# Heads' stage of a hybrid decoder layer: results stored at once, their sums in the decay tiles of the ended scan, a third output gate buffer, gate pieces one tile later

## The chip, the cores and the metric

The kernel runs on one core of one Trainium2 chip. The metric is the device time of one execution in microseconds (us), taken as the median of three timed runs; lower is better. One further execution was taken with the hardware profiler, and every duration of a single instruction comes from that one.

A core has five engines that run their own instruction streams and wait for each other by semaphores: TensorE (PE in the profile; PEld is its weight load), VectorE (DVE), ScalarE (ACT), GpSimd (POOL) and SyncE (SP), which here issues nearly all DMAs. An engine takes its instructions in the order written down for it, so one that waits holds up all behind it.

## What is computed

The reference is one decoder layer on 512 tokens of width 2048 in float32. A normalized, conditioned input `h` is multiplied by one wide matrix `w_in`; its slices feed a sliding-window attention branch (a) and a gated DeltaNet branch (b), which are gated, added, and projected by `w_out`. The change lies in branch b. Cut to what matters:

```python
d_qkv = causal_conv_silu(d_qkv, conv_w)
dq, dk, dv = jnp.split(d_qkv, [DN_KEY, 2 * DN_KEY], axis=-1)
dq = jnp.repeat(l2_norm(dq...), rep, axis=2)      # 16 key heads, 32 value heads, 128 wide
dk = jnp.repeat(l2_norm(dk...), rep, axis=2)
o = gated_delta_rule(dq, dk, dv, g, beta)         # a scan over chunks with a 128x128 state per head
o = rms_norm(o, dn_norm_w) * jax.nn.silu(dz...)   # dz: the output gate
y_b = o.reshape(B, T, DN_VAL) @ w_o_dn            # 512x4096 by 4096x2048
y = jax.nn.sigmoid(mg_a) * y_a + jax.nn.sigmoid(mg_b) * y_b
return x + gate * (y @ w_out)                     # gate: c @ w_ada, last third
```

## The kernel before

**Matrix work.** Every float32 product is made of three passes of a rounded format (`mm3`, lines L275 to L277): the weights are split by ScalarE into a high part (`whi`, L53) and by VectorE into the rest (`wlo`, L54). `channel_tile` makes one tile of 128 channels by 512 tokens: 16 slices of the input's width, 48 matmuls, about 11 us. After every second slice it calls `pump`, eight times a tile.

**Side work.** All else is written as Python generators. `go` puts one among the live ones; every `pump` lets each live generator whose count has run out take its next step, and a `yield n` means "n pumps later" (`JOIN` in a yield puts the step beside another one's small matmuls). `beside(gen, rate, queue)` adds a queue that takes `rate` steps per pump. The program so written is then put in order for each engine by a list scheduler: an instruction can stand earlier or later than it was written, as its inputs are reckoned to be ready. `behind()` pins what is written inside it to a place after the latest matmul, without any wait on the chip.

**The heads' stage** runs from about 500 to 1650 us. `heads` (L889) takes the 16 key heads in turn, each with its pair of value heads, as five channel tiles: one of queries (`q`), two of values (`v`), two of the output gate (`z`). After the 16 pairs come two more channel tiles (`ma3`, `ma4`, part of the merge gates), then `drain_live`, which lets the last generators finish, then `drain` of the two side queues (L695 to L697).

- `queries` loads two decay tiles `E` (called `M` there; four buffers, 128 x 512 each) from `g_rows`, turns them into the masked decay, and multiplies them into the products of queries and keys; `values` transposes the values (`ptv`, L309).
- `scan` (L1010 on) runs the four chunks of the pair: `pp`, `r`, `pv`, `vn`, `vs`, `pd`, `S`, `po`. ScalarE copies `vn` (L1028) out of PSUM, VectorE scales it to `vs` (L1033), TensorE makes `pd` from it (L1041). The scan of one pair ends during the tiles of the next. Then the output is scaled (`osb`, L1077), transposed (`pto`) and multiplied into the gate tile (L1086): `z[e]` holds the result.
- `zgate` (L902) takes a gate tile `zh` from a ring of two buffers, writes it by ScalarE (L905), then makes `zth` (L907) and the silu (L909).
- `head_sums` (L1091) makes what the next stage needs. That stage multiplies by `w_o_dn` in seven block products instead of eight (a scheme of Strassen's kind), for which the four blocks of the left side (two heads, tokens 0 to 255 as `lo` and 256 to 511 as `hi`) and three sums of them, plus one that replaces a block, go to the scratch tensor `oq_d` in seven places. `od_order` says which product reads which place.

**The next stage** (`branch_b`) starts with two merge-gate tiles and then reads `oq_d` (`oraw`, L1123), splits it (`oh`, `ol`), and multiplies (`od`).

**The gate queue.** From the ninth pair (g = 8) on, the queue "gate" runs `gate` (L1653), which makes the vector `gate` of the reference: 32 pieces, each one VectorE operation over 1024 columns (L1670, L1672) with a load of 512 KB (`gw`) three pieces ahead, then four ends, each a load of `b_gate` (`gb`), a matmul (`pgate`, L1680), two VectorE operations (L1682, L1683) and a store. `heads` sets its rate: 0 in the query tile and the first value tile, 0.22 per pump in the second value tile and both gate tiles. From g = 2 on another queue ("ws") adds weight blocks in memory with large DMAs.

Of the kernel before, what the change touches and what calls it, by code (L numbers as in the profile page):

```python
# [7 lines left out]
F32 = mybir.dt.float32  # L8
# [3 lines left out]
ALU = mybir.AluOpType  # L12
# [4 lines left out]
P = 128  # L17
T = 512
# [19 lines left out]
class Layer:  # L38
# [670 lines left out]

    def od_order(self):  # L710
        return [
            ("m1", 0, (0, 0)), ("m2", 2, (1, 0)), ("m5", 4, None), ("m6", 5, None), ("m7", 1, None), ("m4", 3, None),
            ("m3", 6, (1, 1)),
        ]

# [173 lines left out]
    def heads(self, wk, g):  # L889

        st = {"z": []}
        for q in self.side.get("gate", []):
            q[1] = 0.0
        self.go(self.queries(wk, g, self.channel_tile(f"q{g}"), st), 0)
        for e in range(2):
            for q in self.side.get("gate", []) if e else []:
                q[1] = 0.22
            self.go(self.values(wk, g, e, self.channel_tile(f"v{2 * g + e}"), st), 0)
        for e in range(2):
            self.go(self.zgate(wk, self.channel_tile(f"z{2 * g + e}"), st), 0)  # L900

    def zgate(self, wk, ps, st):  # L902
        nc = self.nc
        zh = wk.tile([P, T], F32, tag="z", name="zh", bufs=2)
        nc.scalar.activation(zh, ps, AF.Copy, scale=self.dnwh)  # L905
        th = wk.tile([P, T], F32, tag="th", name="zth")
        nc.scalar.activation(th, ps, AF.Tanh, scale=0.5)  # L907
        yield 1
        nc.vector.scalar_tensor_tensor(out=zh, in0=th, scalar=1.0, in1=zh, op0=ALU.add, op1=ALU.mult)  # L909
        st["z"].append(zh)  # L910
# [95 lines left out]
    def scan(self, wk, g, k, kT, TT, qd, M, epsq, st):  # L1006
        nc = self.nc
# [5 lines left out]
        for c in range(NTB):  # L1013
            if c:
# [3 lines left out]
                for e in range(2):  # L1018
                    nc.vector.scalar_tensor_tensor(
                        out=r[:, e, :], in0=pp[:, e, :], scalar=self.neg_eg[:, c, 2 * g + e : 2 * g + e + 1],  # L1020
                        in1=v[e][:, c, :], op0=ALU.mult, op1=ALU.add,
# [8 lines left out]
            if c < NTB - 1:  # L1030
                vs = wk.tile([P, 2, P], F32, tag="vs", name="vs", bufs=1)
                for e in range(2):
                    nc.vector.tensor_scalar(  # L1033
                        out=vs[:, e, :], in0=vn[:, e, :], scalar1=self.kd[:, c, 2 * g + e : 2 * g + e + 1],
# [16 lines left out]
            if c < NTB - 1:  # L1051
# [3 lines left out]
                else:  # L1055
                    for e in range(2):
                        nc.vector.scalar_tensor_tensor(
                            out=Sn[:, e, :], in0=S[:, e, :], scalar=self.egl[:, c, 2 * g + e : 2 * g + e + 1],
                            in1=pd[:, e, :], op0=ALU.mult, op1=ALU.add,
# [4 lines left out]
        z = st["z"]  # L1064
# [4 lines left out]
        for e in range(2):  # L1069
            nc.vector.scalar_tensor_tensor(  # L1070
                out=ms[:, e, :], in0=osq[:, e, :], scalar=1.0 / P, in1=epsq, op0=ALU.mult, op1=ALU.add
# [3 lines left out]
        for e in range(2):  # L1075
            of = osb[:, e]
            nc.vector.tensor_tensor(  # L1077
                out=of, in0=of, in1=ro[:, e * NTB : (e + 1) * NTB].unsqueeze(2).to_broadcast([P, NTB, P]), op=ALU.mult
# [6 lines left out]
        for e in range(2):  # L1085
            nc.vector.tensor_tensor(out=z[e], in0=pts[e], in1=z[e], op=ALU.mult)  # L1086
            yield 1
        yield 5
        yield from self.head_sums(wk, g, z)

    def head_sums(self, wk, g, z):  # L1091

        nc = self.nc
        TT, STT = nc.vector.tensor_tensor, nc.vector.scalar_tensor_tensor
        lo, hi = slice(0, 256), slice(256, 512)
        s = wk.tile([P, 3, 256], F32, tag="sums", name="zs", bufs=1)
        TT(out=s[:, 0], in0=z[0][:, hi], in1=z[1][:, hi], op=ALU.subtract)
        STT(out=s[:, 1], in0=s[:, 0], scalar=-1.0, in1=z[0][:, lo], op0=ALU.mult, op1=ALU.subtract)
        yield 1
        TT(out=z[0][:, hi], in0=z[0][:, lo], in1=z[0][:, hi], op=ALU.add)  # L1100
        STT(out=s[:, 2], in0=s[:, 1], scalar=-1.0, in1=z[1][:, lo], op0=ALU.mult, op1=ALU.subtract)
        yield 3
        two = lambda x: x.rearrange("p (q t) -> p q t", q=2)
        for q, src in ((slice(0, 2), two(z[0])), (slice(2, 4), two(z[1])), (slice(4, 7), s)):
            nc.sync.dma_start(out=self.oq_d[q, g // 2].rearrange("q p k t -> p q k t")[:, :, g % 2, :], in_=src)


    def branch_b(self):
# [657 lines left out]
```

## Time and profile before

| what | us |
|---|---|
| median of three runs | 2892.06 |
| lowest and highest run | 2890.61, 2895.87 |
| the profiled execution | 2897.53 |
| its span, first to last instruction | 2895.8 |
| TensorE busy in it | 2832.1 |
| VectorE busy | 1875.7 |
| ScalarE busy | 1141.0 |

The time of an execution is its span and what lies around it, here 1.7 us. In a row of the timeline stand the start, the duration, the engine, the line of the kernel, the operation, the tiles (written <- read), the shapes, the number of instructions merged, and in brackets how long the engine stood idle before it and what ended that. In a row of waits stand who waited for whom, the total, the times, and the longest. "SPq" is SyncE issuing a DMA. Matmuls overlap in the pipeline, so the duration of one is longer than its share of the time.

### The profile page before, as it was taken

The numbers are of one execution on the slowest core, as the hardware profiler recorded it, in microseconds if no ns is written. First come the engines' busy times: TensorE is split into PE (matmuls) and PEld (weight loads), VectorE is DVE, ScalarE is ACT, GpSimd is POOL, SyncE is SP. The second block draws the span as 40 slices with busy tenths as digits, with TensorE's granted clock in tenths as the row PEclk, the third lists the DMA queues.
The fourth block names the chain that finished last, engine by engine and source line by source line (L and its number), as shares of the span: only waits on it lengthen the run. The fifth ranks groups of instructions, "written<-read, shape, count | busy, mean of one in ns | idle before, by whom it ended". The sixth has DMA issues, their size and how long they took to land.

```text
span 2895.8 us, 38255 instructions
## 1 busy us (share of the span) xinstructions
PE 2832.1 (98%) x14428; PEld 2328.1 (80%) x14428; DVE 1875.7 (65%) x3020; ACT 1141.0 (39%) x2161; POOL 281.8 (10%) x266
## 2 busy tenths in 40 slices
PE   8899999999999999999999999999999999999999
PEld 6677888888888788888878788888887788788787
DVE  6765898778787556666655456665555655554565
ACT  4354333433334333333333354443334434442343
POOL 0022111111111111111110000000100100000000
PEclk9999999999999999999999999999999999999999
DMA  9757564646667768878863377676645547365575
GB/s 386 289 164 206 168 183 144 207 129 218 189 203 207 232 197 265 242 241 235 250 171 107 130 252 264 241 249 208 219 152 162 160 152 213 124 226 179 188 232 168
DMA packets 205473, 590.09 MB, mean 204 GB/s; under 512 B 74564, under 2 KB 99652, under 8 KB 154088
## 3 DMA queue, kind: packets, MB, share of 16 engines
q1 hardware_dynamic: 195080, 529.44, 53.6%
q0 software_dynamic: 10208, 58.20, 10.3%
q8 instruction: 113, 1.85, 0.3%
q14 instruction: 72, 0.59, 0.1%
HBM read 523.79 MB, written 166.40 MB: 238 GB/s over the span
## 4 chain that ended last, share of the span: by engine, by line
PE 83%; DMA 4%; DVE 3%; issue 2%; ACT 1%; POOL 0%; SPq 0%; DVEq 0%; POOLq 0%; ACTq 0%
PE mm L275 19%; PE mm L277 19%; PE mm L276 19%; PE od L276 3%; PE od L275 3%; PE od L277 3%; DMA oq_d<-zh 2%; PE m L276 2%; PE m L277 2%; PE m L275 2%; PE S L1404 1%; PE po L1045 1%; PE O L1455 1%; PE pv L1026 1%; PE pP L309 1%
## 5 line engine op out<-in xcount | busy, mean ns | idle before, releaser
L275 PE MATMUL mm<-hh,whi 128*128 128x512 f32 x2784 | 1126.8, 405 | 2.3 <-ACT whi L53 1.6
L277 PE MATMUL mm<-hh,wlo 128*128 128x512 f32 x2784 | 1089.3, 391 | 1.1 <-DVE wlo L54 1.1
L276 PE MATMUL mm<-hl,whi 128*128 128x512 f32 x2784 | 1087.8, 391 | 0.0
L54 DVE TENSOR_TENSOR wlo<-raw,whi 128x1024 fp32r<-128x1024 f32 (+1 forms) x476 | 588.9, 1240 | 421.0 <-ACT whi L53 419.6
L53 ACT CAST whi<-raw 128x1024 fp32r<-128x1024 f32 (+1 forms) x476 | 496.8, 1047 | 776.3 <-PE mm L276 657.9
L275 PEld LDWEIGHTS mm<-hh,whi 128*128 128x128 f32 x2784 | 524.5, 188 | 115.2 <-issue 9.6
L277 PEld LDWEIGHTS mm<-hh,wlo 128*128 128x128 f32 x2784 | 523.2, 188 | 114.6 <-DVE wlo L54 1.9
L276 PEld LDWEIGHTS mm<-hl,whi 128*128 128x128 f32 x2784 | 524.7, 188 | 101.4 <-issue 1.4
L276 PE MATMUL od<-wlo,oh 128*128 128x512 f32 x448 | 174.5, 390 | 0.8 <-DVE wlo L54 0.8
L275 PE MATMUL od<-whi,oh 128*128 128x512 f32 x448 | 174.8, 391 | 0.0
L277 PE MATMUL od<-whi,ol 128*128 128x512 f32 x448 | 174.4, 389 | 0.0
L813 POOL TENSOR_TENSOR E<-E,neg_g 128x512 f32<-128x512 f32 x64 | 90.5, 1414 | 475.6 <-DMA E<-g_rows 339.2
L972 POOL TENSOR_TENSOR qe<-qe,yq 128x512 f32<-128x512 f32 x32 | 49.6, 1567 | 880.1 <-DMA qe<-eg_rows 654.4
L865 DVE TENSOR_TENSOR A<-A,atmp 128x62 f32<-128x62 f32 (+30 forms) x124 | 112.6, 908 | 1.4
L858 DVE TENSOR_TENSOR atmp<-A 128x62 f32<-128x62 f32 (+30 forms) x124 | 110.3, 890 | 1.3
L276 PEld LDWEIGHTS od<-wlo,oh 128*128 128x128 f32 x448 | 84.1, 188 | 18.2 <-DVE wlo L54 1.2
L277 PEld LDWEIGHTS od<-whi,ol 128*128 128x128 f32 x448 | 84.1, 188 | 17.5
L275 PEld LDWEIGHTS od<-whi,oh 128*128 128x128 f32 x448 | 84.1, 188 | 17.2
L54 DVE TENSOR_TENSOR wlo<-raww,whi 128x1024 fp32r<-128x1024 f32 x56 | 68.4, 1223 | 44.4 <-ACT whi L53 44.4
L53 ACT CAST whi<-raww 128x1024 fp32r<-128x1024 f32 x56 | 58.9, 1056 | 79.5 <-PE m L277 71.7
L1047 ACT COPY osb<-po 128x256 f32<-128x256 f32 x64 | 23.9, 373 | 149.7 <-PE po L1045 149.7
L1428 ACT ACTIVATE sm<-sm,mx,rs 128x256 f32<-128x256 f32 (+1 forms) x128 | 72.1, 565 | 3.3 <-DVE mx L1423 3.3
(341 smaller groups left out, 3288.7 us busy)
## 6 DMA issues: line engine op xcount, KB each, us to landing
raw<-in_w_ch SPq DMA_DIRECT2D x158, 1024.0 KB
wa<-in_w_ada_ss SPq DMA_DIRECT2D x32, 1024.0 KB
od_m<-in_w_od POOLq DMA_DIRECT2D x32, 1024.0 KB, 13.9
raw<-od_m SPq DMA_DIRECT2D x32, 1024.0 KB
raw<-in_w_od SPq DMA_DIRECT2D x24, 1024.0 KB
E<-g_rows SPq DMA_DIRECT2D x64, 256.0 KB
od_m<-in_w_od SPq DMA_DIRECT2D x16, 1024.0 KB
od_m<-od_m SPq DMA_DIRECT2D x16, 1024.0 KB
```

What stands on the lines that cost most here:

```text
L53: self.nc.scalar.copy(out=hi, in_=src)
L54: self.nc.vector.tensor_tensor(out=lo, in0=src, in1=hi.bitcast(F32), op=ALU.subtract)
L275: nc.tensor.matmul(ps, lhsT=wh, rhs=xh, start=first, stop=False)
L276: nc.tensor.matmul(ps, lhsT=wh, rhs=xl, start=False, stop=False)
L277: self.last_mm = nc.tensor.matmul(ps, lhsT=wl, rhs=xh, start=False, stop=last).ins
L309: self.small = self.nc.tensor.transpose(dst[:, c * P : (c + 1) * P], src_cols(c), self.ident).ins.name
L813: self.in_turn(nc.gpsimd.tensor_tensor(out=E, in0=E, in1=ng, op=ALU.add))
L858: eng.tensor_tensor(out=t, in0=A[:, m : m + 1, m + 1 :].to_broadcast([P, m, n]), in1=A[:, :m, m : m + 1].to_broadcast([P, m, n]), op=ALU.mult,
L865: eng.tensor_tensor(out=A[:, :m, m + 1 :], in0=A[:, :m, m + 1 :], in1=t, op=ALU.add)
L972: self.in_turn(nc.gpsimd.tensor_tensor(out=qf, in0=qf, in1=q, op=ALU.mult))
L1026: nc.tensor.matmul(pv[:, e, :], lhsT=TT[e][:, c, :], rhs=r[:, e, :] if c else v[e][:, c, :], start=True, stop=True)
L1428: nc.scalar.activation(t, t, AF.Exp, scale=r[:, h : h + 1], bias=mx[:, h : h + 1], accum_out=den[:, h : h + 1])
```

## The change

Four things change, all in the heads' stage.

1. `zgate` has three buffers for `zh`, not two.
2. `head_sums` stores at once, one pump step after the multiplications, what the next stage reads as it is: `z[0]`'s first half, and `z[1]`.
3. The sums are no longer made in a tile of their own and partly over `z[0]`, but in the pair's two decay tiles `M`, whose scan is over. They come seven pump steps later, pinned behind a matmul, and are stored three steps after that. There are four stores a pair instead of three, of the same seven places; the places in `oq_d` are numbered anew, and `od_order` follows.
4. The rate of the queue of gate pieces is set to 0 ahead of the value tiles and to 0.22 ahead of the two gate tiles. It thus holds in the gate tiles and in the next pair's query tile; in the query tile of the ninth pair the queue's first rate, 0.125, stands.

```diff
     def od_order(self):
         return [
-            ("m1", 0, (0, 0)), ("m2", 2, (1, 0)), ("m5", 4, None), ("m6", 5, None), ("m7", 1, None), ("m4", 3, None),
+            ("m1", 0, (0, 0)), ("m2", 1, (1, 0)), ("m5", 3, None), ("m6", 4, None), ("m7", 5, None), ("m4", 2, None),
             ("m3", 6, (1, 1)),
         ]
...
         st = {"z": []}
-        for q in self.side.get("gate", []):
-            q[1] = 0.0
         self.go(self.queries(wk, g, self.channel_tile(f"q{g}"), st), 0)
         for e in range(2):
-            for q in self.side.get("gate", []) if e else []:
-                q[1] = 0.22
+            for q in self.side.get("gate", []):
+                q[1] = 0.0
             self.go(self.values(wk, g, e, self.channel_tile(f"v{2 * g + e}"), st), 0)
+        for q in self.side.get("gate", []):
+            q[1] = 0.22
         for e in range(2):
             self.go(self.zgate(wk, self.channel_tile(f"z{2 * g + e}"), st), 0)
...
-        zh = wk.tile([P, T], F32, tag="z", name="zh", bufs=2)
+        zh = wk.tile([P, T], F32, tag="z", name="zh", bufs=3)
...
-        yield 5
-        yield from self.head_sums(wk, g, z)
-
-    def head_sums(self, wk, g, z):
+        yield from self.head_sums(g, z, M)
+
+    def head_sums(self, g, z, s):
 
         nc = self.nc
         TT, STT = nc.vector.tensor_tensor, nc.vector.scalar_tensor_tensor
         lo, hi = slice(0, 256), slice(256, 512)
-        s = wk.tile([P, 3, 256], F32, tag="sums", name="zs", bufs=1)
-        TT(out=s[:, 0], in0=z[0][:, hi], in1=z[1][:, hi], op=ALU.subtract)
-        STT(out=s[:, 1], in0=s[:, 0], scalar=-1.0, in1=z[0][:, lo], op0=ALU.mult, op1=ALU.subtract)
+        two = lambda x: x.rearrange("p (q t) -> p q t", q=2)
+        s = [x.rearrange("p c i -> p (c i)") for x in s]
+
+        def store(q, src):
+            nc.sync.dma_start(out=self.oq_d[q, g // 2].rearrange("q p k t -> p q k t")[:, :, g % 2, :], in_=src)
+
         yield 1
-        TT(out=z[0][:, hi], in0=z[0][:, lo], in1=z[0][:, hi], op=ALU.add)
-        STT(out=s[:, 2], in0=s[:, 1], scalar=-1.0, in1=z[1][:, lo], op0=ALU.mult, op1=ALU.subtract)
+        store(slice(0, 1), z[0][:, lo].unsqueeze(1))
+        store(slice(1, 3), two(z[1]))
+        yield 7
+        with self.behind():
+            TT(out=s[0][:, lo], in0=z[0][:, hi], in1=z[1][:, hi], op=ALU.subtract)
+            STT(out=s[0][:, hi], in0=s[0][:, lo], scalar=-1.0, in1=z[0][:, lo], op0=ALU.mult, op1=ALU.subtract)
+        yield 1
+        with self.behind():
+            TT(out=s[1][:, lo], in0=z[0][:, lo], in1=z[0][:, hi], op=ALU.add)
+            STT(out=s[1][:, hi], in0=s[0][:, hi], scalar=-1.0, in1=z[1][:, lo], op0=ALU.mult, op1=ALU.subtract)
         yield 3
-        two = lambda x: x.rearrange("p (q t) -> p q t", q=2)
-        for q, src in ((slice(0, 2), two(z[0])), (slice(2, 4), two(z[1])), (slice(4, 7), s)):
-            nc.sync.dma_start(out=self.oq_d[q, g // 2].rearrange("q p k t -> p q k t")[:, :, g % 2, :], in_=src)
+        store(slice(3, 5), two(s[0]))
+        store(slice(5, 7), two(s[1]))
```

## The prediction

> **What bounds the kernel now.** The first part of the page gives each engine's share:
>
> ```profile
> span 2895.8 us, 38255 instructions
> PE 2832.1 (98%) x14428; PEld 2328.1 (80%) x14428; DVE 1875.7 (65%) x3020; ACT 1141.0 (39%) x2161; POOL 281.8 (10%) x266
> ```
>
> TensorE is busy for 2832.1 of 2895.8 us. The change takes no matrix work away, so it can win only TensorE's idle time and its half-clock time, and only in the stage that it touches. That stage is read next from the view of windows (us, then busy time of TensorE and the others, granted clock, DMA share, GB/s). The first four rows cover all heads, the last two are close looks:
>
> ```profile
> 560.00:960.00 400.00, 399.73 (x2117) 334.92 (x2116) 312.49 (x506) 156.81 (x342) 50.47 (x44) 1.00 0.63 189
> 960.00:1230.00 270.00, 266.99 (x1410) 223.48 (x1409) 158.76 (x272) 98.75 (x223) 41.40 (x40) 0.99 0.78 234
> 1230.00:1640.00 410.00, 396.79 (x2082) 329.26 (x2082) 245.99 (x414) 143.05 (x317) 47.30 (x40) 0.99 0.63 189
> 1640.00:1660.00 20.00, 16.27 (x69) 13.42 (x68) 8.82 (x24) 5.30 (x13) 0.00 (x0) 0.83 0.49 164
> ...
> 992.00:999.00 7.00, 4.18 (x17) 3.47 (x16) 1.69 (x5) 1.87 (x5) 0.00 (x0) 0.76 0.33 118
> 1463.00:1473.00 10.00, 3.88 (x12) 3.02 (x11) 3.89 (x6) 3.40 (x9) 0.00 (x0) 0.66 1.02 319
> ```
>
> Idle TensorE: 0.3 + 3.0 + 13.2 + 3.7 = 20.2 us. That is nearly the whole prize. The waits of TensorE from 560 to 1640 us (total, times, longest) name its parts:
>
> ```profile
> PE pd L1041 <- DVE vs L1033: 11.7, 5, 6.1
> PE ptv L309 <- DVE yv L623: 2.7, 4, 1.5
> PE ptv L309 <- DVE E L978: 2.1, 1, 2.1
> ```
>
> So 11.7 us are scan steps (`pd`) that wait for VectorE's `vs`, and 4.8 us are value transposes (`ptv`) that wait for VectorE. The timeline at the largest `pd` wait shows who is really late:
>
> ```profile
> 1467.11 0.69 ACT L905 ACTIVATE zh<-mm,dnwh 128x512 f32<-128x512 f32 x1 [10.17 <-DMA oq_d<-zh]
> ...
> 1468.17 0.37 ACT L1028 COPY vn<-pv 128x256 f32<-128x256 f32 x1
> ...
> 1469.46 1.22 PE L1041 MATMUL pd<-vs,k 128*128 128x256 f32 x2 [6.12 <-DVE vs L1033]
> ```
>
> ScalarE stands 10.17 us at L905 because both gate buffers of `zh` still hold the results of the pair before, whose store to `oq_d` has not landed. Behind it in ScalarE's order are `zth` and `vn`; `vs` needs `vn`, and `pd` needs `vs`. TensorE loses 6.12 of the 10.17. Over the program the wait and the landings (from the chain of waits: start, length) are:
>
> ```profile
> ACT zh L905 <- DMA oq_d<-zh: 37.2, 9, 10.2
> ```
>
> ```profile
> 982.80 10.37 DMA oq_d<-zh
> 1308.98 13.78 DMA oq_d<-zh
> 1377.44 14.92 DMA oq_d<-zh
> 1447.07 19.93 DMA oq_d<-zh
> ```
>
> A store takes 10 to 20 us to land here, and 37.2 us of ScalarE's waits become 11.7 us on TensorE: (37.2 - 11.7) / 9 = 2.8 us of each are absorbed on average.
>
> **The change part by part.** *Third gate buffer and storing at once.* The SyncE rows of the same pair:
>
> ```profile
> 1447.07 0.38 SPq L1105 DMA_DIRECT2D oq_d<-zh  x1
> ...
> 1458.12 5.87 SPq L1105 DMA_DIRECT2D oq_d<-zs  x1
> ```
>
> The store issued at 1447.07 is that of `z[1]`, which the sums never overwrite, and the wait ended on its landing at 1467.0. So it already goes out at once, and the new order of the stores alone would not cure this wait; the third buffer does. With it the first gate tile of the next pair (due at 1467.11 - 10.17 = 1456.94) takes a free buffer, and only the second needs one of these results. It is due a tile later, 12.7 us by the first two gate tiles, which waited for nothing:
>
> ```profile
> 572.68 0.68 ACT L905 ACTIVATE zh<-mm,dnwh 128x512 f32<-128x512 f32 x1
> ...
> 585.42 0.68 ACT L905 ACTIVATE zh<-mm,dnwh 128x512 f32<-128x512 f32 x1
> ```
>
> That makes about 1469.7, later than even this slowest landing by 2.7 us. The sums read `z` until 9 to 10 pump steps after the multiplication (1.4 us of matmuls each, some 14 us with the small ones: 1460), so they release in time too. I therefore take the whole 11.7 us. Bounds: 11.7, or nothing if landings reach over 23 us.
>
> *Clock.* The close looks at 992 and 1463 us grant 0.76 of 7 us and 0.66 of 10 us: 1.7 and 3.4 us missing. In the second, the idle time ends at 1469.46, so about half of the 3.4 fell into it. I take 1.7 + 1.8 = 3.5 us more. The Trainium skill, "TensorE: Matmul & The Clock Gate", Why this matters for your kernels, asks for no idle gaps over about 3 us; by that the gap of 7.00 - 4.18 = 2.8 us at 992 costs no clock, and the sum is 1.7 us smaller. The trace's 0.76 contradicts it.
>
> *Gate pieces out of the second value tile, sums pinned later.* In the new code the rate is set to 0 only ahead of the value tiles and to 0.22 ahead of the gate tiles, so it stays at 0.22 through the next pair's query tile: 24 pumps a pair as before, in `z`, `z`, `q` instead of `v`, `z`, `z`. VectorE's load in a second value tile and in the query tile after it:
>
> ```profile
> 1292.00:1302.40 10.40, 10.40 (x53) 8.80 (x53) 10.33 (x10) 3.07 (x6) 9.27 (x7) 1.00 1.00 276
> 1333.00:1346.40 13.40, 13.40 (x69) 11.33 (x68) 5.06 (x11) 4.59 (x11) 0.00 (x0) 1.00 0.66 239
> ```
>
> VectorE is full for 10.33 of 10.40 us in the first and for 5.06 of 13.40 us in the second. What stood ahead of the `ptv` wait that followed at 1314 us:
>
> ```profile
> 1302.92 2.07 DVE L1672 SCALAR_TENSOR_TENSOR gate_bc<-gw,silu_c,gate_bc 128x1024 f32<-128x1024 f32 x1
> ...
> 1311.71 0.41 DVE L1097 TENSOR_TENSOR zs<-zh 128x256 f32<-128x256 f32 x1
> ...
> 1313.37 0.41 DVE L1101 SCALAR_TENSOR_TENSOR zs<-zs,zh 128x256 f32<-128x256 f32 x1
> ...
> 1314.84 0.68 DVE L623 SCALAR_TENSOR_TENSOR yv<-th,yv 128x512 f32<-128x512 f32 x1
> ```
>
> A piece of the value tile (2.07 us) and four sums (4 x 0.41 = 1.6 us) leave this place, 3.7 us for a wait of about 1.5 us; a piece of the gate tile itself stays. The groups by line from 1100 to 1640 us (busy, mean ns, idle before) have the waits of the pairs with gate pieces:
>
> ```profile
> L309 PE MATMUL ptv<-ident,yv 128*128 128x128 f32 x64 | 9.8, 276 | 4.5 <-DVE yv L623 2.4 <-DVE E L978 2.1
> ```
>
> Of these 4.5 us I count 4 as gone; bounds 0 and 4.8. In the query tile two pieces, 4.1 us at 2.07 each, find 8.3 us of idle VectorE: nothing. Without that they would cost 4.1 us in each of seven query tiles, 29 us. The sums, 0.8 us at a time, stand later in the first gate tile, before a `vs` that has 2.8 us to spare: nothing; without that cover 16 x 1.6 = 26 us. The gate queue needs 41 steps (one to start, 32 products, 8 for its four ends). Before, the 41st comes at pump 187 of 192; now 8 pumps at 0.125 give one and 182 at 0.22 give 40, so it ends in the last pair's second gate tile in both, and nothing is left for the end of the stage. There the idle 3.7 us stay, too: the last scan has no matrix work to hide behind.
>
> *Sums in the decay tiles.* This is the new wait. The decay tiles of pair g are the ones into which the loads of pair g + 2 go. Today these are issued as soon as the scan's last `po` is done; the mask follows 10 us later, the exponential only after 73 us:
>
> ```profile
> 1288.22 0.39 PE L1045 MATMUL po<-vn,E 128*128 128x128 f32 x2
> ...
> 1288.85 0.90 SPq L806 DMA_DIRECT2D E<-g_rows  x2
> ...
> 1298.72 1.96 POOL L813 TENSOR_TENSOR E<-E,neg_g 128x512 f32<-128x512 f32 x1
> ...
> 1307.68 1.27 DVE L1086 TENSOR_TENSOR zh<-pto,zh 128x512 f32<-128x512 f32 x2
> ...
> 1362.36 1.17 ACT L966 ACTIVATE E<-E 128x512 f32<-128x512 f32 x2
> ```
>
> From now on they wait until the sums are made (some 12 us after the multiplication at 1307.7, about 1320) and have landed (10 to 20 us: 1330 to 1340). Load to mask takes 1298.7 - 1288.9 = 10 us, the masks of GpSimd some 7 us: ready at 1347 to 1357, before ScalarE's exponential at 1362. So the data come in time, by 5 us at worst. But SyncE may stand at this load for the landing, 10 to 20 us in every pair. Queued behind it are weight loads:
>
> ```profile
> 1322.82 0.35 SPq L235 DMA_DIRECT2D raw<-in_w_ch  x1
> ...
> 1327.51 0.33 SPq L235 DMA_DIRECT2D raw<-in_w_ch  x1
> ...
> 1345.61 1.05 ACT L53 CAST whi<-raw 128x1024 fp32r<-128x1024 f32 x1 [0.78 <-PE mm L276]
> ...
> 1360.33 1.04 ACT L53 CAST whi<-raw 128x1024 fp32r<-128x1024 f32 x1
> ```
>
> The load at 1327.5 is issued 33 us before its split; held until 1340 it still has 20 us, and the one with 23 us had no DMA wait. The gate pieces' loads run three pieces ahead, some 20 us. I take 1 us in all; ends 0 and 42 (14 pairs reload these tiles, 3 us each, what a `zh` wait of 6 us costs after the 2.8 that are absorbed). The value is near the lower end, because the two nearest rows show the lead. One more store per pair is 16 x 0.38 = 6 us of SyncE beside those leads, and the new places in `oq_d` move the same bytes: nothing.
>
> **Sum.** -11.7 - 3.5 - 4 + 1 = -18.2 us. Against the profiled execution (2897.5 us, of which 2895.8 span) that is 2879.3. The median before is 2892.06, 5.5 us below the profiled one. If this difference is profiling, the new median is 2874; if it is more of the same DMA waits, they vanish and 2879 holds. I take 2880, as landings are what varies.
>
> **Rivals.** (a) *The wait moves instead of going, and the change does not do what it says.* The second gate tile waits for the same stores, and the 11.7 + 3.5 us stay; only the 4 us of `ptv` are won, less 1: 2889 against the median. It decides once landings exceed 23 us. For it: the margin is 2.7 us at 1447, and SyncE hung 5.87 us in one issue. Against: the three other landings are 10 to 15 us. (b) *SyncE stands at the reload of the decay tiles.* With 3 us a pair on TensorE, 42 us come in and 19.2 are won: 2892 + 23 = 2915. From 19.2 / 14 = 1.4 us a pair on it is no gain any more. For it: SyncE already stands at loads of the same place for `po`, and a held weight load would stop ScalarE, with `vn` behind it, as `zh` does today. Against: the leads above. The waits of SyncE have
>
> ```profile
> SPq L951 <- PE po L1044: 38.4, 14, 16.0
> ```
>
> The Trainium skill, "DMA: Bandwidth & Descriptors", Anatomy of one DMA, says that DMA engines never wait on semaphores and the issuing sequencer does, before it dispatches. The trace agrees (38.4 us in 14 waits of SyncE itself). The same page's fixed 2.0 us per DMA would hold SyncE for under 3 us a pair and leave nothing of (b); landings of 10 to 20 us contradict it.
>
> **Chances.** Forecast 0.66, around 2880 (own range 2872 to 2886); (a) 0.17; (b) 0.17. About 0.2%, 5.8 us, is what a measurement can tell from no change: faster 0.66, same 0.17, slower 0.17. The range 2872 to 2896 holds most of the forecast and (a) and the mildest of (b).
>
> **What would show it.** Right: the wait of `zh` for `oq_d` gone from ScalarE's waits, `pd` without waits, clock 1.00 in the windows from 960 to 1640 us, `ptv` waits under 1 us in sum. Wrong: L905 still waiting for stores at every second tile (a); long SyncE waits of the load of `E` for `oq_d`, then `whi` or `gate_bc` waiting for DMA (b). An idle sum in the heads much above 5 us would break the forecast.

## The result and the profile after

The changed kernel takes 2883.29 us in the median of seven runs (2880.61 to 2886.63), the kernel before 2893.24 us (2890.61 to 2895.87): ratio 0.9966, 95% interval 0.9954 to 0.9978, so 9.95 us or 0.34% faster. A second sitting (`x3_after_again`, below) gave 0.9953 with 0.9940 to 0.9965. The prediction said 2880.0, 2872 to 2896, faster.

The head of the page of the changed kernel's profiled execution (2886.63 us):

```profile
span 2884.9 us, 38287 instructions
PE 2832.8 (98%) x14428; PEld 2329.4 (81%) x14428; DVE 1857.8 (64%) x3020; ACT 1139.0 (39%) x2161; POOL 272.5 (9%) x266
```

TensorE is as busy as before (2832.1 us then), in a span that is 10.9 us shorter. The windows of the heads (us, then busy time of TensorE, its weight loads, VectorE, ScalarE, GpSimd, granted clock, DMA share, GB/s) show where it was won:

```profile
560.00:960.00 400.00, 396.56 (x2096) 331.70 (x2095) 302.19 (x498) 155.97 (x342) 47.04 (x43) 1.00 0.62 185
960.00:1230.00 270.00, 270.00 (x1432) 226.50 (x1432) 156.26 (x283) 99.97 (x224) 36.73 (x37) 1.00 0.81 243
1230.00:1640.00 410.00, 403.99 (x2121) 336.20 (x2120) 246.26 (x429) 147.25 (x325) 47.24 (x43) 1.00 0.64 192
1640.00:1660.00 20.00, 19.96 (x85) 16.29 (x84) 10.56 (x18) 8.10 (x12) 0.00 (x0) 0.91 0.73 226
```

Idle TensorE is now 3.4 + 0 + 6.0 + 0.04 = 9.5 us, where it was 20.2. The first window got worse, by 3.2 us: there are two new waits in it. The waits from 560 to 1640 us, of TensorE and of ScalarE (total, times, longest):

```profile
PE pd L1041 <- DVE vs L1033: 5.7, 3, 2.5
PE pto L309 <- DVE osb L1077: 3.7, 1, 3.7
```

```profile
ACT E L966 <- POOL E L815: 14.7, 5, 4.8
ACT atmp L870 <- DMA ta_d<-atmp: 4.8, 3, 3.3
```

ScalarE no longer waits for `oq_d` at all, and the `ptv` waits are gone. But three scan steps still wait, 5.7 us in sum, and these are not those of before. The timeline of one of them (start, length, engine, line; in brackets the idle time before it and its releaser), with the stores of the sums and the load of a decay tile ahead of it:

```profile
1524.25 0.38 SPq L1099 DMA_DIRECT2D oq_d<-E  x1
...
1525.55 0.40 SPq L1099 DMA_DIRECT2D oq_d<-E  x1
...
1526.47 3.82 SPq L806 DMA_DIRECT2D E<-g_rows  x2
...
1535.52 1.05 POOL L813 TENSOR_TENSOR E<-E,neg_g 128x512 f32<-128x512 f32 x1 [1.74 <-DMA E<-g_rows]
...
1536.64 0.64 POOL L815 TENSOR_SCALAR_AFFINE_SELECT E<-E 128x512 f32<-128x512 f32 x1
...
1537.31 0.63 ACT L966 ACTIVATE E<-E 128x512 f32<-128x512 f32 x1 [2.86 <-POOL E L815]
...
1538.79 0.68 ACT L905 ACTIVATE zh<-mm,dnwh 128x512 f32<-128x512 f32 x1
...
1539.84 0.37 ACT L1028 COPY vn<-pv 128x256 f32<-128x256 f32 x1
...
1541.19 0.70 PE L1041 MATMUL pd<-vs,k 128*128 128x256 f32 x2 [2.29 <-DVE vs L1033]
```

Read it from the end: `pd` waits for `vs`, `vs` for `vn`, and `vn` stands in ScalarE's order behind the next gate tile (`zh`) and the exponential of a decay tile, which waits for GpSimd's mask, which waits for the reload, which waits for the sums' stores. So the sums in the decay tiles do cost something. The same chain ends in a wait of 0.92 us at 658.7 us. The third wait, 2.52 us at 928.5, has ScalarE standing 3.26 us at the copies that end the second solve (`atmp`, L870), for the store of an earlier copy.

### The profile page after: what moved, and what is told of

Its sections match the earlier page's. It is cut to its first block, busy times and chain, and to the rows that moved or that the text cites. A ratio compares the mean times of both kernels' runs of the same rounds, so it can differ in the third digit from the quotient of the medians.

```text
span 2884.9 us, 38287 instructions
## 1 busy us (share of the span) xinstructions
PE 2832.8 (98%) x14428; PEld 2329.4 (81%) x14428; DVE 1857.8 (64%) x3020; ACT 1139.0 (39%) x2161; POOL 272.5 (9%) x266
## 4 chain that ended last, share of the span: by engine, by line
PE 87%; DVE 2%; issue 2%; DMA 1%; ACT 0%; SPq 0%; POOL 0%; DVEq 0%; POOLq 0%; ACTq 0%
PE mm L275 21%; PE mm L277 20%; PE mm L276 20%; PE od L276 3%; PE od L275 3%; PE od L277 3%; PE m L276 2%; PE m L277 2%; PE m L275 2%; PE S L1413 1%; PE po L1045 1%; PE O L1464 1%; PE pv L1026 1%; PE pP L309 1%; PE po L1044 1%
## 5 line engine op out<-in xcount | busy, mean ns | idle before, releaser
L813 POOL TENSOR_TENSOR E<-E,neg_g 128x512 f32<-128x512 f32 x64 | 79.8, 1248 | 946.6 <-DMA E<-g_rows 721.1
## 6 DMA issues: line engine op xcount, KB each, us to landing
od_m<-in_w_od POOLq DMA_DIRECT2D x32, 1024.0 KB, 10.7
```

Source lines behind the costliest of these rows:

```text
L813: self.in_turn(nc.gpsimd.tensor_tensor(out=E, in0=E, in1=ng, op=ALU.add))
```

## The experiments

**Theory 1**, as the prediction had it: the third buffer removes the wait of `zh`, worth 11.7 us and clock beside it; the gate pieces bring 4 us of `ptv`; the order of the stores alone nothing. **Theory 2**: it is VectorE's relief, from gate pieces and sums, that gets the stores out in time. The first four runs do one part alone, or leave one part out. Ratios are to the kernel before on the same chip.

### Third buffer alone

```
-zh = wk.tile([P, T], F32, tag="z", name="zh", bufs=2)
+zh = wk.tile([P, T], F32, tag="z", name="zh", bufs=3)
...
-th = wk.tile([P, T], F32, tag="th", name="zth")
+th = wk.tile([P, T], F32, tag="th", name="zth", bufs=1)
```

(and the same single buffer for `th` in the convolutions of this stage; by the two lines that this takes, the lines of the heads stand two lower)

> The kernel before with a third gate buffer and nothing else of the change (the tile of the tanh, tag th, has one buffer in place of two to make room). Theory 1, the third buffer is the cure: the wait of zh for oq_d falls from 37.2 us to under 2 us, the waits of pd for vs from 11.7 to under 2 us, the ptv waits stay near 4.8 us; time 2893 - 11.7 to 15 = 2878 to 2882 us. Theory 2, VectorE's relief (gate pieces and sums out of the second value tile) is the cure: the store goes out as late as before, the second gate tile now waits for it, pd still waits some 8 to 12 us; time 2889 to 2893 us.

Measured: 2880.54 us, ratio 0.9949 (0.9937 to 0.9961). TensorE's waits in the heads:

```profile
PE pto L309 <- DVE osb L1079: 3.7, 1, 3.7
PE ptv L309 <- DVE yv L623: 2.6, 5, 1.1
PE ptv L309 <- DVE E L980: 1.8, 1, 1.8
```

No `pd` row is left, no `zh` wait either, and the `ptv` waits stay at 4.4 us. Theory 1 sized this part rightly. By its ratio this part alone already gives as much as the whole change (0.9966 and 0.9953 in two sittings).

### Gate pieces alone

```
 self.go(self.queries(...), 0)
 for e in range(2):
-    for q in self.side.get("gate", []) if e else []:
-        q[1] = 0.22
+    for q in self.side.get("gate", []):
+        q[1] = 0.0
     self.go(self.values(...), 0)
+for q in self.side.get("gate", []):
+    q[1] = 0.22
```

> The kernel before with nothing but the gate pieces moved out of the second value tile. Theory 1: the wait of zh for oq_d stays at 30 to 40 us and the pd waits at 8 to 13 us, only the ptv waits of the pairs with gate pieces (4.5 us) go; time 2888 to 2891 us. Theory 2: with VectorE free in the second value tile the multiplications and stores go out earlier, the zh wait falls under 15 us; time 2882 to 2885 us.

Measured: 2879.64 us, ratio 0.9945 (0.9932 to 0.9957). With two gate buffers, and stores and sums as before:

```profile
PE pd L1041 <- DVE vs L1033: 2.5, 2, 2.2
PE ptv L309 <- DVE yv L623: 0.3, 1, 0.3
```

```profile
ACT zh L905 <- DMA oq_d<-zh: 19.5, 6, 6.2
```

Theory 1 expected 2888 to 2891 here and missed by 8 us. Not only the `ptv` waits went, as it had said, but 9.2 of the 11.7 us of `pd` as well, although ScalarE still waits 19.5 us for stores. Theory 2 missed too: it wanted the `zh` wait under 15 us and a time of 2882 to 2885.

### Two buffers, the rest of the change

```
-zh = wk.tile([P, T], F32, tag="z", name="zh", bufs=3)
+zh = wk.tile([P, T], F32, tag="z", name="zh", bufs=2)
```

> The changed kernel with two gate buffers in place of three: stores at once, sums in the decay tiles, gate pieces shifted. Theory 1: the wait of zh for oq_d is back, and longer than the 37.2 us of before, as the sums that read z stand 16 us behind the multiplication (40 to 100 us), pd waits 12 to 30 us; time 2893 to 2915 us. Theory 2: it stays within 3 us of the changed kernel, 2881 to 2886 us.

Measured: 2881.96 us, ratio 0.9953 (0.9941 to 0.9966).

```profile
PE pd L1041 <- DVE vs L1033: 4.0, 5, 1.4
```

```profile
ACT zh L905 <- DVE E L1110: 24.5, 9, 3.4
```

The wait is back in ScalarE, mostly for the sums that read the old gate results, and it is not felt: at most 3.7 us each time (10.7 us more, in three waits, are put down to other releasers). TensorE's five `pd` waits stand elsewhere: four behind the exponential of a decay tile or the copies of the second solve, the fifth (0.26 us) behind VectorE's own work. That ends theory 1 as a whole: without the buffer the time is the same.

### Third buffer and stores, gate pieces as before

```
+for q in self.side.get("gate", []):
+    q[1] = 0.0
 self.go(self.queries(...), 0)
 for e in range(2):
-    for q in self.side.get("gate", []):
-        q[1] = 0.0
+    for q in self.side.get("gate", []) if e else []:
+        q[1] = 0.22
     self.go(self.values(...), 0)
-for q in self.side.get("gate", []):
-    q[1] = 0.22
```

> The changed kernel with the gate pieces where they were before (second value tile and both gate tiles). Theory 1: zh does not wait for oq_d, pd waits stay near the 5.7 us of the changed kernel, 4 to 5 us of ptv waits come back; time 2886 to 2889 us. Theory 2: the gain is gone, 2890 to 2894 us.

Measured: 2881.41 us, ratio 0.9949 (0.9935 to 0.9962), `pd` waits 3.5 us, no `ptv` wait in the list. Both theories missed. Against the third buffer alone, which keeps 4.4 us of `ptv` waits, this kernel differs in the stores and sums, so moving the sums out of the second value tile is enough for `ptv`, as moving the gate pieces out was above. Each part alone gives at least as much as the whole change, and leaving one out loses nothing. The parts are substitutes, and the next question is of what.

### Loads of the gate pieces left out

Of the 32 loads of gate weights three are made, and the products read these again, so another gate is computed.

```
-s = self.sc[:, i // 2 : i // 2 + 1]
+s, w = self.sc[:, i // 2 : i // 2 + 1], ws.pop(i)
...
 if i + 3 < 2 * KT:
-    load(i + 3)
+    ws[i + 3] = w
```

> The kernel before, but of the 32 loads of gate weights only the first three are made; the 32 gate products read these again (the gate is therefore another one), at the same places and with the same work for VectorE. Theory A, the store of z lands late because the gate pieces' loads of 512 KB stand ahead of it in the DMA queues: the zh waits from pair 9 on (3.9, 3.6, 4.7, 10.2 us) shrink to under 3 us each, the pd waits after 1230 us (8.7 us) to under 2 us, the ptv waits stay near 4.8 us; time 2881 to 2885 us. Theory B, VectorE's work in the second value tile makes the multiplication and with it the store late: zh and pd waits stay within 3 us of before; time 2890 to 2895 us.

Measured: 2885.28 us, ratio 0.9960 (0.9947 to 0.9972). `pd` waits 4.5 us, `zh` waits 26.9 us. At the place of the longest wait:

```profile
1442.73 1.27 DVE L1086 TENSOR_TENSOR zh<-pto,zh 128x512 f32<-128x512 f32 x2
...
1459.57 0.69 ACT L905 ACTIVATE zh<-mm,dnwh 128x512 f32<-128x512 f32 x1 [5.68 <-DMA oq_d<-zh]
...
1461.91 0.70 PE L1041 MATMUL pd<-vs,k 128*128 128x256 f32 x2 [1.62 <-DVE vs L1033]
```

Without the loads the buffer comes free 16.8 us after the start of the multiplication; before, 1467.11 - 1445.77 = 21.3 us (the multiplication of that pair is in the row below). So 4.5 us of this landing went with the loads, of 512 KB each. In the kernel with the gate pieces alone no such load is issued in the 22 us ahead of this store, and the gate tile starts 15.3 us after the multiplication.

```profile
1445.77 1.27 DVE L1086 TENSOR_TENSOR zh<-pto,zh 128x512 f32<-128x512 f32 x2
```

Theory A was right for the longest wait, and in part for the rest: the waits from pair 9 on are 2.4, 2.1, 4.0 and 5.7 us, not all under 3, the `pd` waits after 1230 us are 2.7 us, not under 2, and the time is just above its range. Beside the second profile of the kernel before (3.1, 2.2, 4.6 and 9.7 us, last run below) only the longest is clearly shorter.

### Stores at once and sums in the decay tiles

The kernel "third buffer and stores, gate pieces as before" with two gate buffers. It has points 2 and 3 of the change together; no run has the new order of the stores with the sums where they were.

```
-zh = wk.tile([P, T], F32, tag="z", name="zh", bufs=3)
+zh = wk.tile([P, T], F32, tag="z", name="zh", bufs=2)
```

> Of the change only the stores at once and the sums in the decay tiles: two gate buffers, gate pieces as before. If the order of the stores alone does not cure the wait, as the prediction said: zh waits 35 us or more in all, pd waits 10 us or more in the heads; time 2889 to 2900 us. If it cures the wait, since nothing but the reads of the sums (about 16 us behind the multiplication) then holds a gate buffer: zh waits of about 2.5 to 4 us a pair that TensorE does not feel, pd waits 2 to 6 us; time 2880 to 2885 us.

Measured: 2881.05 us, ratio 0.9954 (0.9940 to 0.9967). The same place:

```profile
1434.88 1.28 DVE L1086 TENSOR_TENSOR zh<-pto,zh 128x512 f32<-128x512 f32 x2
...
1454.40 0.69 ACT L905 ACTIVATE zh<-mm,dnwh 128x512 f32<-128x512 f32 x1 [6.63 <-DMA oq_d<-zh]
...
1456.75 0.70 PE L1041 MATMUL pd<-vs,k 128*128 128x256 f32 x2 [2.58 <-DVE vs L1033]
```

The rows of this place in three kernels give what the prediction lacked. ScalarE's wait less TensorE's is 10.17 - 6.12 = 4.05 us before, 5.68 - 1.62 = 4.06 without the loads, 6.63 - 2.58 = 4.05 here: whatever the wait, its first 4.05 us at this place are free. Another place has another margin, and keeps it too: in the kernel before

```profile
993.25 0.69 ACT L905 ACTIVATE zh<-mm,dnwh 128x512 f32<-128x512 f32 x1 [4.17 <-DMA oq_d<-zh]
...
995.60 1.22 PE L1041 MATMUL pd<-vs,k 128*128 128x256 f32 x2 [2.82 <-DVE vs L1033]
```

only 4.17 - 2.82 = 1.35 us are free (2.75 - 1.40 = 1.35 without the loads). The due time (when ScalarE could have started the gate tile) is 1456.94 - 1445.77 = 11.2 us behind the start of the multiplication before, 1453.89 - 1442.73 = 11.2 without the loads, but 1447.77 - 1434.88 = 12.9 us here, since the multiplication has moved ahead. Here the buffer comes free 19.5 us behind the multiplication instead of 21.3, and the tile is due 1.7 us later: the wait falls by 3.5 us, and so does TensorE's. In the other pairs ScalarE still waits, mostly for the sums (39.3 us in all, more than before), but no other `pd` wait stands behind it:

```profile
ACT zh L905 <- DVE E L1110: 21.8, 8, 3.6
...
ACT zh L905 <- DMA oq_d<-zh: 10.3, 2, 6.6
ACT zh L905 <- PE pv L1026: 7.2, 2, 3.7
```

The gate pieces alone fit: their longest wait, 6.22 us at 982 us, costs TensorE 2.16, again 4.06 less. The kernel before has that margin there too (4.24 and 0.19).

### Third buffer and gate pieces, stores and sums as before

```
-zh = wk.tile([P, T], F32, tag="z", name="zh", bufs=2)
+zh = wk.tile([P, T], F32, tag="z", name="zh", bufs=3)
...
-    for q in self.side.get("gate", []) if e else []:
-        q[1] = 0.22
+    for q in self.side.get("gate", []):
+        q[1] = 0.0
...
+for q in self.side.get("gate", []):
+    q[1] = 0.22
```

(`th` with one buffer, as in the third buffer alone)

> The kernel before with the third gate buffer and the shifted gate pieces, stores and sums as before (tag th with one buffer, to make room). No zh wait, no pd wait, no ptv wait but 0.3 us; of the idle time in the heads only the 3.7 us of the last pair are left; time 2875 to 2879 us, and faster than the changed kernel by 3 to 6 us if the sums in the decay tiles are what still costs there. If the changed kernel's waits have another cause: pd waits of 3 us or more, 2880 us or more.

Measured: 2876.23 us, ratio 0.9929 (0.9917 to 0.9942), five runs of 2874.32 to 2879.22.

```profile
PE pto L309 <- DVE osb L1079: 3.7, 1, 3.7
PE ptv L309 <- DVE yv L623: 0.3, 1, 0.3
```

Only the last pair's idle time is left. The two parts are worth 2897.13 - 2876.23 = 20.9 us together, 14.6 and 15.5 alone (both against 2895.15).

### The changed kernel again, on the same chip

No edit.

> The changed kernel as it is, on the same chip as the three others. If its 2883.3 us is its own time: 2882 to 2886 us with before at 2893 to 2896, pd waits 4 to 6 us, two of them behind the exponential of the decay tile. If the earlier sitting was a little slow: 2879 to 2882 us, the same as each part alone.

Measured: 2882.84 us, ratio 0.9953 (0.9940 to 0.9965), five runs of 2881.74 to 2885.79, none as fast as the slowest of the kernel just shown.

```profile
PE pd L1041 <- DVE vs L1033: 5.9, 3, 2.8
```

So the stores and sums of the change, once the two other parts are there, make it 6.6 us slower. The other difference, one buffer for `th`, shows no new wait in ScalarE's list.

### Sums earlier

```
 store(slice(1, 3), two(z[1]))
-yield 7
+yield 1
...
-yield 3
+yield 1
 store(slice(3, 5), two(s[0]))
```

> The changed kernel with its sums 6 pump steps earlier (about 8 us) and their stores 2 steps earlier, so that the decay tiles are released some 10 us earlier. If the reload of the decay tiles is what makes TensorE wait near 657 and 1536 us (1.0 and 2.1 us, exponential behind GpSimd's mask behind the load): both go, and half of the half-speed clock behind the second; pd waits 2.8 us instead of 5.9; time 2876 to 2880 us beside 2883 for the changed kernel. If the exponential is early in ScalarE's order for another reason: both stay within 1 us, 2881 to 2885 us.

Measured: 2875.79 us, ratio 0.9934 (0.9922 to 0.9947).

```profile
PE pd L1041 <- DVE vs L1033: 0.2, 1, 0.2
```

The two waits behind the reload are gone, but for 0.2 us, as expected of that cause. The third, at the solve's copies, went with them, which was not expected (2.8 us were to stay).

### Copies of the solve further apart

```
 nc.sync.dma_start(out=rows[:, q * 512 : (q + 1) * 512], in_=t)
+yield 4.0
```

> The changed kernel with the eight copies at the end of each solve (atmp, stored to ta_d) 4 us further apart, so that a copy no longer waits for the store of the one two before. If ScalarE's wait for ta_d is what makes TensorE wait near 927 us (2.8 us): it goes, pd waits about 3 us instead of 5.9; time 2879 to 2882 us. If not, within 1 us of the changed kernel.

Measured: 2882.66 us, ratio 0.9957 (0.9944 to 0.9969).

```profile
PE pd L1042 <- DVE vs L1034: 3.0, 2, 2.1
```

The wait near 927 us is gone as expected; the time is not shorter, against 2879 to 2882 us expected. From its first gate tile to the start of the last multiplication by `pto` it took 1060.1 us, 3.2 less than the changed kernel's second profile (1063.3), but its first gate tile came 3.4 us later (576.6 against 573.2 us). In the kernel with the earlier sums, on the same chip and with no edit ahead of this point, the first gate tile was as late (576.5). So as a time this run decides nothing; as a cause of that wait the copies are shown.

### Both

> The changed kernel with both edits, sums early and copies paced. If the two causes are all that the changed kernel still loses: pd waits under 1 us, only the 3.7 us of the last pair idle; 2875 to 2878 us, the same as third buffer and gate pieces alone (2876.2). If something else remains: 2879 us or more.

Measured: 2877.59 us, ratio 0.9938 (0.9925 to 0.9952). TensorE's list of waits in the heads has one row:

```profile
PE pto L309 <- DVE osb L1078: 3.7, 1, 3.7
```

Nothing else remains, as expected. Pacing the copies adds nothing measurable to the earlier sums.

### The kernel before, a second profile

No edit.

> The kernel before as it is, for a second profile. If its waits are its own and not those of one execution: zh waits for oq_d of 30 to 42 us, pd waits of 9 to 14 us, the longest again near 1463 us; ratio 1.000 within 0.15%. If they vary between executions: pd waits under 7 us.

Measured: ratio 1.0002 (0.9993 to 1.0010).

```profile
PE pd L1041 <- DVE vs L1033: 9.3, 4, 5.6
```

```profile
ACT zh L905 <- DMA oq_d<-zh: 33.3, 9, 9.7
```

The waits belong to the kernel, not to one execution; the `pd` waits vary by 2.4 us, those of `zh` by 3.9.

All runs together; the medians come from several sittings, so compare the ratios:

| kernel | median us | ratio to before | `pd` waits us | `zh` waits for stores or sums, us |
|---|---|---|---|---|
| before (first / second profile) | 2893.24 / 2895.99 | 1 / 1.0002 | 11.7 / 9.3 | 37.2 / 33.3 |
| third buffer alone | 2880.54 | 0.9949 | 0 | 0 |
| gate pieces alone | 2879.64 | 0.9945 | 2.5 | 19.5 |
| stores at once and sums in the decay tiles | 2881.05 | 0.9954 | 5.0 | 21.8 (sums), 10.3 (stores) |
| all but the third buffer | 2881.96 | 0.9953 | 4.0 | 24.5 (sums) |
| all but the gate pieces | 2881.41 | 0.9949 | 3.5 | 0 |
| the whole change | 2883.29 / 2882.84 | 0.9966 / 0.9953 | 5.7 / 5.9 | 0 |
| third buffer and gate pieces | 2876.23 | 0.9929 | 0 | 0 |
| the whole change, sums earlier | 2875.79 | 0.9934 | 0.2 | 0 |
| the whole change, copies further apart | 2882.66 | 0.9957 | 3.0 | 0 |
| the whole change, both | 2877.59 | 0.9938 | 0 | 0 |
| before, gate loads left out | 2885.28 | 0.9960 | 4.5 | 26.9 |

## Why the prediction was right, and where it was not

**The prize** was right: the heads' idle time was what could be won, and the best kernels win all of it but the 3.7 us of the last pair, which stayed as the prediction said.

**The wait of `zh`** went completely, and the buffer alone takes 11.7 us of `pd` waits to nothing, as step one said. **The sentence beside it misled:** "the new order of the stores alone would not cure this wait; the third buffer does". At that place a wait of 6.63 us is indeed left without the buffer, so the sentence itself isn't refuted; but the buffer isn't needed for most of the gain, since stores and sums together gave 0.9954. The step looked at when the store is issued and when it lands, but not at the margin. At the longest wait 4.05 us are free and at another 1.35, where the prediction had 2.8 us for all, from sums divided over nine waits of several lengths; and the other parts move due time and landing by a few us each, which takes most of what exceeds the margin. For the same reason the 4 us of the gate pieces were far too few alone (15.5 us), and the gains of parts measured alone can't be added.

**The reload of the decay tiles** is the term that was mis-sized: +1 us by the prediction, some 6 us by the runs (2882.84 against 2876.23 us without the stores and sums, 6.6; the ratios 0.9953 and 0.9934 with and without the late sums, 5.5). It had been read from one pair, whose exponential followed its load after 73 us. In pairs 2 and 15 (g = 2 and g = 15; in the other reloads it is 48 us or more) ScalarE's order has it much earlier; the kernel before shows that in its own timeline:

```profile
611.33 0.90 SPq L806 DMA_DIRECT2D E<-g_rows  x2
...
620.60 0.64 ACT L966 ACTIVATE E<-E 128x512 f32<-128x512 f32 x1 [5.58 <-POOL E L815]
...
1503.50 0.90 SPq L806 DMA_DIRECT2D E<-g_rows  x2
...
1512.62 0.63 ACT L966 ACTIVATE E<-E 128x512 f32<-128x512 f32 x1 [4.79 <-POOL E L815]
```

Nine us behind the load, and ScalarE already waited there. That wait cost TensorE nothing, since no `vn` stood close behind it. In the changed kernel it isn't even longer (2.99 and 2.86 us in pair 15, against 4.79 and 1.63), but there the load goes out after the sums, the exponential stands among the gate tiles, and `vn` behind it comes too late. The data themselves came sooner than forecast: in pair 15 the masks were ready 29 us after the start of the multiplication, where the prediction has 39 to 49. So what failed is the due time, not the landing. Listing all 16 loads against their exponentials would have shown it. Rival (b) had the right resource and the wrong victim. SyncE does stand there,

```profile
SPq L806 <- DMA oq_d<-E: 35.5, 15, 7.1
```

but at 35.5 / 15 = 2.4 us a time, where the prediction feared 10 to 20, and no weight load came late for it; the data themselves did.

**Clock**: -3.5 us predicted. Close looks at the changed kernel grant 0.79 of 8 us twice, 1.7 us missing each time:

```profile
928.00:936.00 8.00, 5.48 (x22) 4.47 (x21) 1.08 (x4) 4.22 (x10) 0.32 (x1) 0.79 0.54 166
1538.00:1546.00 8.00, 5.71 (x21) 4.42 (x21) 2.83 (x6) 3.66 (x10) 0.00 (x0) 0.79 0.00 0
```

Before, 1.7 + 3.4 = 5.1 us were missing, 3.5 of them outside the idle time; here it is 3.4, all behind the new gaps. So nearly nothing was won in this execution. In the second profile of the changed kernel nothing is missing at these places (last section), and the 3.5 were won. **Value transposes**: -4 predicted, -4.8 measured. **Gate queue and extra store**: no tail, no new wait, as said. **Sum**: -6.0 for `pd` (-11.7 + 5.7), -0.1 clock, -4.8 `ptv` are -10.9 us against -18.2. Measured from the first gate tile to the last pair's multiplication it is

```profile
575.08 0.68 ACT L905 ACTIVATE zh<-mm,dnwh 128x512 f32<-128x512 f32 x1
...
1640.44 1.36 DVE L1086 TENSOR_TENSOR zh<-pto,zh 128x512 f32<-128x512 f32 x2
```

1065.4 us, where the kernel before takes 1649.61 - 572.68 = 1076.9:

```profile
1649.61 0.69 DVE L1086 TENSOR_TENSOR zh<-pto,zh 128x512 f32<-128x512 f32 x1 [0.61 <-PE pto L309]
```

That is -11.6 us; the stages ahead are 2.4 us longer and those behind 1.7 us shorter in this execution, and the span is 10.9 us shorter. So the time came out 3.3 us from the forecast with the prize rightly sized and one cost put at 1 us in place of some 6. Part of that closeness is luck: the 18.2 us were taken off a profiled execution that ran 5.5 us above the median. Taken off the median of 2892.06 they give 2873.9, 9.4 us too low. And of the prediction's own signs only some came: no `zh` wait, no `ptv` wait and a granted clock that rounds to 1.00 from 960 to 1640 us, but `pd` still waits, and TensorE's idle sum of 9.5 us is well above the 5 us that it named as the limit. That the causes were alternatives didn't disturb the forecast, which counted the wait once; it would have ruined one for the gate pieces alone or the stores and sums alone (2888 to 2900 us expected, 2880 to 2881 measured). **Rival (a)** did not happen: no gate tile waits for a store.

What stays open is why ScalarE's order has the exponential early in just these two pairs. How the earlier sums also cure the wait at the solve's copies is not shown by a run of its own, but the kept traces point to the reload again. In the changed kernel the loads of the decay tiles go out at 917.99 and 920.11 us, among the stores of the copies; the store at 921.01 us holds up the copy that starts at 929.17, 8.2 us later. With the sums early the loads go out at 913 us, ahead of the first of these stores (916.67), and that copy starts 5.3 us after its store was issued (920.58), without a wait; in the kernel before it is 5.6 us. No run moved the load alone.

## What to carry to other kernels

Before adding up the parts of a change, write for each wait its release, its due time and what it may be late for free; parts that each take most of the same excess are substitutes, and one alone wins most of it (14.6 or 15.5 us here, 20.9 for two together). When a buffer gets a second use, check the distance from its reload to the first reader in every round of the loop, not in one, and what stands behind that reader on its engine. Then try the change without its costly part: here two of the three parts are 6.6 us faster than all three.

## What the runs showed of the hardware

At one place a landing followed the traffic ahead of it: the same 256 KB store released its buffer 21.3 us after the start of the multiplication (20.9 in the second profile), and 16.8 us when the loads of 512 KB were left out. The stores of the sums, some 16 us behind the multiplication, let the reload go 2.2 us after the first of them was issued in the quickest pairs (1524.25 to 1526.47 us in the rows above) and 9.7 us in the slowest of the 14.

The clock does not answer to a gap's length alone. In the changed kernel gaps of 2.52 and 2.29 us were each followed by a stretch with 0.79 granted over 8 us (above). In its second profile gaps of 2.76 and 2.07 us at the same places cost no clock:

```profile
926.00:934.00 8.00, 5.24 (x29) 4.18 (x27) 1.09 (x4) 5.14 (x10) 0.51 (x1) 1.00 0.50 144
1535.00:1543.00 8.00, 5.93 (x30) 4.45 (x28) 4.05 (x7) 3.69 (x10) 0.00 (x0) 1.00 0.00 0
```

Over all profiles there are nine gaps of 2.06 to 2.82 us before a `pd`; half clock followed four of them (2.82, 2.52, 2.29, 2.16) and not the other five (2.76, 2.58, 2.46, 2.07, 2.06). It followed the 3.7 us of the last pair in all 14 profiles.

So the rule of about 3 us in the Trainium skill, "TensorE: Matmul & The Clock Gate", Why this matters for your kernels, held in one execution and not in the other; a forecast should carry such a clock term as a maybe.
